# Forgetting attention of a decoder trunk: the queries' head norm moves from a multiply of the queries into the scale of the softmax exponential, and three query tiles move behind the first two heads' scores

## The chip, the cores and the metric

The kernel runs on one core of a Trainium2 chip. The metric is the device time of one execution in microseconds (us), lower is better. One core has a TensorE (PE, with its weight loads shown apart as PEld), a VectorE (DVE), a ScalarE (ACT), a GpSimd (POOL) and a SyncE (SP), which here issues nearly all DMAs in one queue. Each engine runs its own instructions strictly in the order in which they were written to it, and waits on semaphores for the others.

## The reference, cut to what matters

Two layers of a decoder trunk are computed for 512 prompt tokens and 8 x 4 sample tokens (T = 544 columns), width 1024, 8 heads of 128. The second layer mixes with forgetting attention:

```
q = rmsnorm((xn @ att_w_q).reshape(L, 8, 128), q_norm)      # per token and head
s = einsum('bqhd,bkhd->bhqk', q, k) * 128 ** -0.5
s = s + cq[..., :, None] - csum[..., None, :]               # running sums of log forget values
s = where(causal, s, -inf)
p = softmax(s, axis=-1)
o = einsum('bhqk,bkhd->bqhd', p, v);  mix = o @ att_w_o
```

The sample tokens do the same against 256 past keys per stream and their own 4 new ones, with the forget term as an additive bias.

## The kernel before

All activations lie transposed: 128 features on the partitions, 544 tokens along the free axis. A matrix product takes three passes (high part of the weights by high part of the input, high by low, low by high), so that products come out near fp32; `split_pair` and `prep` make the two parts of an activation (an ACT instruction for the high part, a DVE one for the low part). `ps` are PSUM tiles of two banks (three of them), `pb` tiles of one bank (two), `big` SBUF tiles of 128 x 2 x 544 (45 in a pool), `tmp` tiles of 128 x 544 (8).

The order of the work in the attention is a table, `ORDER`, of small steps; each letter is a function, each digit its head or group. A scheduler then places the instructions of each engine, using the table as priority. The steps that matter here:

- `qN` (`tile`): query tile of head N. Eight blocks of weights, 48 matmuls on 272 columns (L285, L289, L291) into a `ps`. `take` then multiplies by the token's norm on DVE (L1108) and squares on ACT (L786).
- `s0123`, `s4567` (`stat` before): the sums of squares of four heads by matmuls with a block of 32 ones (L794: 4 heads x 2 column halves per group, in fp32), an inverse square root on ACT (L385) with one correction on DVE (L388, L391, L392), four rows written to DRAM (L805) and read back spread over all partitions (L810, one DMA for each head).
- `nN` (`norm` before): DVE multiplies the head's query tile by the gain and that row (L1118).
- `pN` (`prep_q`): high and low part of the prompt columns of the query tile (L329, L330 on `big<-big`).
- `fN` (`fetch`): the head's keys and values from DRAM (L1153, L1154).
- `aN` (`qk`): scores in four blocks of 128 queries against 128 to 512 keys, in two `ps`: a matmul for the forget term (L1169, `L` times `R`), three for q times k (L1170, L1171, L1172) and one for the causal mask (L1174). Then for each block a maximum on DVE (L1184), exp with the maximum as bias and the row sum as second output on ACT (L1185), a reciprocal on DVE (L1186), and the normalisation on ACT for blocks 0 and 3 (L1190) and on POOL for blocks 1 and 2 (L1188).
- `tN` (`turn`): ten transposes of the probabilities (L1200) and their split. `vN` (`pv`): the product with the values (L1219 to L1221) and its split (L1224, L1225).
- `KN`, `VN`: two cache pages of a sample stream; `z` puts the sample queries into a zeroed tile (POOL, L1233), `S0`, `S1` the sample scores (L1246), `T`, `P`, `U`, `O` their softmax and values. `h..`, `o.` the output projection (L1330 to L1337).

The forget term is a matmul with 32 rows for each head: `terms`, made in the K/V stage by `forget`, go through DRAM and `fetch_terms` reads them back. Before, `L` (one tile for each of four heads, refilled for heads 4 to 7) holds the query side and `R` (one tile for all heads) the key side.

## Time and profile before

| what | value |
|---|---|
| median of 3 runs (lowest to highest) | 1928.19 us (1927.69 to 1928.4) |
| the profiled execution | 1928.06 us, of which the profile's span is 1926.3 us |
| busy: PE, DVE, ACT, POOL | 99%, 76%, 49%, 7% of the span |
| first query tile of the attention starts | about 1347.5 us into the span |
| first sample scores (L1246) | 1428.35 us |
| attention's last projections | about 1510 us |

A view named "windows" gives busy time in stretches of the span, "waits" who waited for whom, "timeline" merged instructions in order of time: start, duration, engine, line, operation, tiles, shapes, count, and in brackets the idle time of the engine just before and what ended it. [...] An fp32 matmul that isn't a transpose appears as two MATMUL records.

### The profile page before, as it was taken

The numbers are of one execution on the slowest core, as the hardware profiler recorded it, in microseconds if no ns is written. First come the engines' busy times: TensorE is split into PE (matmuls) and PEld (weight loads), VectorE is DVE, ScalarE is ACT, GpSimd is POOL, SyncE is SP. The second block draws the span as 40 slices with busy tenths as digits, with TensorE's granted clock in tenths as the row PEclk, the third lists the DMA queues.
The fourth block names the chain that finished last, engine by engine and source line by source line (L and its number), as shares of the span: only waits on it lengthen the run. The fifth ranks groups of instructions, "written<-read, shape, count | busy, mean of one in ns | idle before, by whom it ended". The sixth has DMA issues, their size and how long they took to land.

```text
span 1926.3 us, 39008 instructions
## 1 busy us (share of the span) xinstructions
PE 1904.8 (99%) x16508; PEld 1869.8 (97%) x16508; DVE 1457.4 (76%) x1799; ACT 949.2 (49%) x1396; POOL 143.4 (7%) x190
## 2 busy tenths in 40 slices
PE   9999999999999999999999999999999999999999
PEld 8999999999999999999999999999977899999999
DVE  7987877556788887767578887876476888878774
ACT  7544434424554544454466454444374754444461
POOL 0000000410100000023000000002131300000020
PEclk9999999999999999999999999999999999999999
DMA  5233234312223233431484232324769332332431
GB/s 196 90 102 121 89 118 156 99 48 88 89 88 116 91 115 120 132 112 46 149 305 150 98 129 71 128 95 128 226 214 332 99 110 84 109 113 86 140 108 47
DMA packets 98048, 237.62 MB, mean 123 GB/s; under 512 B 12130, under 2 KB 29826, under 8 KB 97874
## 3 DMA queue, kind: packets, MB, share of 16 engines
q1 hardware_dynamic: 97730, 235.09, 36.9%
q8 instruction: 130, 2.13, 0.5%
q14 instruction: 44, 0.36, 0.1%
q10 hardware_dynamic: 144, 0.04, 0.0%
HBM read 218.65 MB, written 16.44 MB: 122 GB/s over the span
## 4 chain that ended last, share of the span: by engine, by line
PE 89%; DVE 5%; ACT 2%; DMA 2%; issue 1%; SPq 0%; POOL 0%; ACTq 0%; DVEq 0%
PE ps L538 31%; PE ps L285 15%; PE ps L291 15%; PE ps L289 15%; PE pb L538 5%; DVE big L242 1%; DMA tmp<-rows 1%; ACT big L241 1%; PE ps L891 1%; PE ps L892 1%; PE ps L893 1%; DVE big L227 1%; DVE big L330 0%; PE ps L1285 0%; PE ps L676 0%
## 5 line engine op out<-in xcount | busy, mean ns | idle before, releaser
L538 PE MATMUL ps<-big,big 128*128 128x272 f32 x5616 | 668.5, 279 | 3.1 <-ACT tmp L546 1.7
L538 PEld LDWEIGHTS ps<-big,big 128*128 128x128 f32 x5616 | 658.4, 189 | 3.9 <-ACT tmp L546 2.1
L242 DVE TENSOR_TENSOR big<-big,big 128x1024 fp32r<-128x1024 f32 (+2 forms) x505 | 582.1, 1156 | 86.7 <-ACT big L241 85.9
L241 ACT CAST big<-big 128x1024 fp32r<-128x1024 f32 (+2 forms) x505 | 482.4, 975 | 325.1 <-DVE big L227 251.5
L285 PE MATMUL ps<-big,big 128*128 128x272 f32 x2668 | 530.1, 280 | 3.0 <-ACT big L241 1.4
L291 PE MATMUL ps<-big,big 128*128 128x272 f32 x2668 | 528.4, 279 | 2.9 <-DVE big L242 2.8
L289 PE MATMUL ps<-big,big 128*128 128x272 f32 x2668 | 527.5, 279 | 0.6 <-DVE big L342 0.6
L285 PEld LDWEIGHTS ps<-big,big 128*128 128x128 f32 x2668 | 407.2, 189 | 7.9 <-ACT big L241 4.5
L291 PEld LDWEIGHTS ps<-big,big 128*128 128x128 f32 x2668 | 406.9, 189 | 5.0 <-DVE big L242 4.5
L289 PEld LDWEIGHTS ps<-big,big 128*128 128x128 f32 x2668 | 406.9, 189 | 1.0 <-DVE big L342 1.0
L370 POOL TENSOR_TENSOR st<-st,tmp 128x544 f32<-128x544 f32 (+1 forms) x63 | 87.4, 1388 | 1472.4 <-ACT tmp L368 1472.1
L227 DVE TENSOR_TENSOR big<-big,big 128x1024 f32<-128x1024 f32 x156 | 190.1, 1219 | 0.0
L577 DVE SCALAR_TENSOR_TENSOR big<-ps,big 128x544 f32<-128x544 f32 x128 | 92.5, 722 | 104.1 <-PE ps L291 103.2
L546 ACT COPY tmp<-ps 128x544 f32<-128x544 f32 x117 | 71.5, 611 | 111.3 <-PE ps L538 111.3
L496 DVE TENSOR_TENSOR big<-big,st 128x1088 f32<-128x1088 f32 x88 | 113.5, 1291 | 3.3 <-ACT big L560 2.0
L538 PE MATMUL pb<-big,big 128*128 128x272 f32 x936 | 114.8, 279 | 0.0
L538 PEld LDWEIGHTS pb<-big,big 128*128 128x128 f32 x936 | 111.3, 189 | 0.0
L499 ACT ACTIVATE big<-big 128x544 f32<-128x544 f32 x88 | 57.8, 659 | 88.0 <-DVE big L496 87.9
L341 ACT ACTIVATE big<-big,gains 128x544 fp32r<-128x544 f32 (+1 forms) x80 | 55.4, 702 | 91.3 <-DVE big L577 55.2
L330 DVE TENSOR_TENSOR big<-big,big 128x544 fp32r<-128x544 f32 (+1 forms) x112 | 79.3, 714 | 22.7 <-ACT big L329 22.5
L342 DVE SCALAR_TENSOR_TENSOR big<-big,gains,big 128x544 fp32r<-128x544 f32 (+1 forms) x80 | 64.6, 817 | 24.3 <-ACT big L341 24.3
L329 ACT CAST big<-big 128x544 fp32r<-128x544 f32 (+1 forms) x112 | 71.2, 643 | 12.2 <-DVE big L502 7.4
(218 smaller groups left out, 1388.5 us busy)
## 6 DMA issues: line engine op xcount, KB each, us to landing
big<-in_w SPq DMA_DIRECT2D x156, 512.0 KB
big<-in_w2b SPq DMA_DIRECT2D x96, 384.0 KB
big<-in_w13p SPq DMA_DIRECT2D x16, 512.0 KB
big<-in_w2a SPq DMA_DIRECT2D x16, 512.0 KB
big<-in_win SPq DMA_DIRECT2D x16, 512.0 KB
big<-in_wg SPq DMA_DIRECT2D x16, 512.0 KB
big<-in_ck SPq DMA_DIRECT2D x16, 512.0 KB
big<-in_cv SPq DMA_DIRECT2D x16, 512.0 KB
```

Of the source, the lines that this page charges most:

```text
L227: self.nc.vector.tensor_tensor(t, a, b, ALU.add if op == "+" else ALU.subtract)
L241: self.nc.scalar.copy(hi, src)
L242: self.nc.vector.tensor_tensor(lo, src, hi.bitcast(F32), ALU.subtract)
L285: i = nc.tensor.matmul(o, wh, xh[:, b], start=s, stop=False)
L289: nc.tensor.matmul(o, wh, xl[:, b], start=False, stop=False)
L291: nc.tensor.matmul(o, wl, xh[:, b], start=False, stop=e)
L330: self.nc.vector.tensor_tensor(pair[:, 1, cols], src, pair[:, 0, cols].bitcast(F32), ALU.subtract)
L370: nc.gpsimd.tensor_tensor(acc[:, cols], acc[:, cols], sq, ALU.add)
L496: tt(g, g, rstd.unsqueeze(1).broadcast_to([P, 2, T]), ALU.mult)
L538: nc.tensor.matmul(turns(dst[w]), a[:, c], woven(b), start=k in "152" and kp == 0 and n == 0, stop=kp == NKP - 1 and n == 2, skip_group_ch ...
L546: nc.scalar.copy(t["r" + k], t["C" if k == "5" else "A"])
L577: nc.vector.scalar_tensor_tensor(halves(h[c]), whole(out), 0.5, halves(h[c]), ALU.mult, ALU.add)
```

## The change

The query tile is no longer normalised. `prep_q` now splits the raw query times the gain. The score matmuls then give q'k without the head norm y (y = 1 / sqrt(sum of squares + 128 eps), which holds the 128 ** -0.5 too), and the exponential multiplies by y, as a scale read per partition: in the scores, queries lie on the partitions. Since y multiplies the forget term as well, that term is divided by y beforehand: `L` holds 1/y of each token and head (high and low part), `R` the negative running sum, one tile for each of four heads.

To have y on the partitions, `stat(g)` takes the sums of squares as columns: for each of four heads and four blocks of 128 tokens one fp32 matmul with the squares as stationary operand and one column of ones as moving operand (L1122), and for group 1 two more for the sample tokens (L1125), whose squares POOL writes. One DVE chain of 15 dependent instructions on 128 x 16 (128 x 18) values follows (bit trick and three Newton steps, then 1/y and its high and low part), and two copies that spread these over a `tmp`. `rows(g)` (step `rN`) turns that by 16 fp32 matmuls with the identity (L1150) and copies it to `L` on ACT (L1152). The rows through DRAM and the eight multiplies of `norm` are gone. In the softmax, blocks go in pairs: two maxima, one multiply of both by the scale, two exps, one reciprocal for both. The gain of the sample queries is applied where they are put into the zeroed tile. Two cache pages (`K1`) are loaded later, and the query tiles 5, 6 and 7 stand after the rows of group 0 and between the first two heads' steps.

```
-q0 K3 K2 K0 q1 q2 q3 K1 s0123 n2 n3 n1 q4 f1 p1 q5 q6 f0 n0 q7 p2 p0 f3 f2 a0 s4567 p3 t0 a1 v0 a2
-t1 n4 n5 a3 n7 n6 t2 p4 z f4 K5 v1 v2 f5 p5 ...
+q0 K3 K2 K0 q1 q2 q3 s0 f0 q4 r0 p0 f1 q5 a0 p1 q6 t0 f2 a1 p2 q7 v0 s1 t1 p3 f3 a2 K1 r1 a3 t2
+p4 z f4 K5 v1 v2 f5 p5 ...
```

```
 forget:
-        act(t1[:, :SEQ], chf, AF.Identity, scale=role(4), bias=role(6))
-        act(t2[:, :SEQ], chf, AF.Identity, scale=role(2), bias=role(7))
-        dve.scalar_tensor_tensor(R[:, 0, :SEQ], clo[:, :SEQ], role(5), t1[:, :SEQ], ALU.mult, ALU.add)
-        dve.scalar_tensor_tensor(t2[:, :SEQ], clo[:, :SEQ], role(3), t2[:, :SEQ], ALU.mult, ALU.add)
+        act(t1[:, :SEQ], chf, AF.Copy, scale=role(4))
+        dve.scalar_tensor_tensor(t1[:, :SEQ], clo[:, :SEQ], role(5), t1[:, :SEQ], ALU.mult, ALU.add)
         for k in range(2):
-            act(L[:, k, :SEQ], t2[:, :SEQ], AF.Copy, scale=role(8 + k))
+            act(R[:, k, :SEQ], t1[:, :SEQ], AF.Copy, scale=role(8 + k))
 stat (new):
+            sq = sqs.pop(4 * g + j)
+            for i in range(4):
+                nc.tensor.matmul(t[:, 4 * j + i:4 * j + i + 1], sq[:, i * P:i * P + P], self.ones[:, 0:1], ...)
+        for k in range(2 * g):
+            nc.tensor.matmul(t[:, 16 + k:17 + k], ss[k], self.ones[:, 0:1], start=True, stop=True)
+        dve.tensor_scalar(x, t[:, :n], P * EPS, None, ALU.add)
+        dve.tensor_scalar(u.bitcast(I32), x.bitcast(I32), 1, None, ALU.logical_shift_right)
+        dve.tensor_scalar(y.bitcast(I32), u.bitcast(I32), -1, 0x5f3759df, ALU.mult, ALU.add)
+        for _ in range(3):
+            dve.tensor_tensor(u, y, y, ALU.mult)
+            dve.scalar_tensor_tensor(u, u, -0.5, x, ALU.mult, ALU.mult)
+            dve.scalar_tensor_tensor(y, u, 1.5, y, ALU.add, ALU.mult)
...
 rows (new):
+        for i in range(4):
+            for j in range(4):
+                nc.tensor.matmul(t[32 * j:32 * j + 32, i * P:i * P + P], w[:, 128 * j + 32 * i:128 * j + 32 * i + 32],
+                                 self.ident, start=True, stop=True, skip_group_check=True)
+        nc.scalar.copy(self.L[:, g, :SEQ], t)
 softmax, block i of head h:
+                if i % 2 == 0:
+                    m2, l2, r2 = self.sm(2), self.sm(2), scale[:, 4 * h + i:4 * h + i + 2]
+                    for k in range(2):
+                        nc.vector.tensor_reduce(m2[:, k:k + 1], S[i // 2][:, k, :w + P * k], AX.X, ALU.max, negate=True)
+                    nc.vector.tensor_tensor(m2, m2, r2, ALU.mult)
-                nc.scalar.activation(blocks_halves(p[:, :w]), blocks_unwoven(sc), AF.Exp, bias=m, accum_out=l)
+                nc.scalar.activation(blocks_halves(p[:, :w]), blocks_unwoven(sc), AF.Exp, bias=m2[:, k], scale=r2[:, k],
+                                     accum_out=l2[:, k])
```

How the instructions move. Rows give line, operation, written tile, read tiles, shape and count; lines of the changed kernel are higher by some 35. On PE, where the fourth query tile ends (its tile is `ps_16502` in both), before:

```order
L291 MATMUL ps_16502<-big_16218,big_16377 128x272 x2
L794 MATMUL pb_16577<-tmp_16385,ones 32x272
L794 MATMUL pb_16577<-tmp_16437,ones 32x272
L794 MATMUL pb_16577<-tmp_16494,ones 32x272
L794 MATMUL pb_16578<-tmp_16385,ones 32x272
L285 MATMUL ps_16615<-big_15943,big_16439 128x272 x2
```

and now, with the fifth query tile in `ps_16601`, its last passes, and the sixth tile in `ps_16687`:

```order
L1122 MATMUL pb_16556<-ones,tmp_16379 128x1 x4
L1122 MATMUL pb_16556<-ones,tmp_16433 128x1 x4
L1122 MATMUL pb_16556<-ones,tmp_16492 128x1 x4
L285 MATMUL ps_16601<-big_15937,big_16437 128x272 x2
...
L1122 MATMUL pb_16556<-ones,tmp_16552 128x1 x4
...
L291 MATMUL ps_16601<-big_16212,big_16438 128x272 x2
L1150 MATMUL pb_16656<-consts,tmp_16588 32x128 x16
L285 MATMUL ps_16687<-big_15937,big_16496 128x272 x2
```

The fourth head's columns stand ten passes into the fifth query tile, and the turn of group 0 (L1150) stands between the fifth and the sixth.

On PE at the second group, before: the last group of ones (L794) stands around the first scores (`ps_16871`, `ps_16872`), ahead of them all:

```order
L1169 MATMUL ps_16872<-big_16225,big_16228 128x384
L794 MATMUL pb_16922<-tmp_16790,ones 32x272
L794 MATMUL pb_16923<-tmp_16790,ones 32x272
L794 MATMUL pb_16922<-tmp_16855,ones 32x272
L794 MATMUL pb_16923<-tmp_16855,ones 32x272
L1170 MATMUL ps_16871<-big_16792,big_16860 128x256
```

and now: the columns of group 1, head 1's transposes (L1241), the scores of heads 2 and 3 (`ps_17074`, `ps_17075` and `ps_17162`, `ps_17163`), the turn of group 1, and head 2's transposes:

```order
L1122 MATMUL pb_17006<-ones,tmp_16986 128x1 x4
L1125 MATMUL pb_17006<-ones,big_16220 128x1 x2
L1241 MATMUL ps_17043<-consts,tmp_16908 128x128
...
L1202 MATMUL ps_17074<-big_16222,big_16219 128x256
...
L1207 MATMUL ps_17163<-neg,identr 128x256
L1150 MATMUL pb_17144<-consts,tmp_17040 32x128 x16
L1241 MATMUL ps_17209<-consts,tmp_17102 128x128
```

The turn of group 1 now stands on PE between the scores of head 3 and the transposes of head 2; no query tile is left behind it.

On DVE in the same stretch, before, maxima, reciprocals and splits follow each other, with one head norm (L1118) among them:

```order
L1225 TENSOR_TENSOR big_17036<-pb_17023,big_17036 128x512
L330 TENSOR_TENSOR big_17102<-ps_17090,big_17102 128x512
L330 TENSOR_TENSOR big_17104<-pb_17091,big_17104 128x256
L1184 TENSOR_REDUCE sm_17143<-ps_17120 128x1
L1186 RECIPROCAL sm_17084<-sm_17084 128x1
L1118 SCALAR_TENSOR_TENSOR big_16664<-big_16664,gains,tmp_17114 128x544
L330 TENSOR_TENSOR big_17103<-ps_17090,big_17103 128x384
```

and now (`cols` is the tile of the chain; nine of its 15 steps stand ahead of these rows):

```order
L330 TENSOR_TENSOR big_17056<-ps_17043,big_17056 128x384
L1219 TENSOR_TENSOR sm_17097<-sm_17097,cols 128x2
L1132 TENSOR_TENSOR cols<-cols 128x18
L342 SCALAR_TENSOR_TENSOR big_17067<-big_16490,gains,big_17067 128x512
L330 TENSOR_TENSOR big_17057<-pb_17044,big_17057 128x128
L1133 SCALAR_TENSOR_TENSOR cols<-cols 128x18
L1134 SCALAR_TENSOR_TENSOR cols<-cols 128x18
L1138 TENSOR_TENSOR cols<-cols 128x16
L1139 CAST cols<-cols 128x16
L1140 TENSOR_TENSOR cols<-cols 128x16
L1144 COPY tmp_17040<-cols 128x128x2
L1218 TENSOR_REDUCE sm_17109<-ps_17075 128x1 x2
```

The chain of group 1 is mixed with the splits of head 1 and the maxima of head 2, and the maxima of head 2's second half (`ps_17075`) stand behind its last step and the first of its two copies.

## The prediction

> **What bounds the kernel now.** I read the page first, then busy time by stretches, then who waits for whom, then PE's instructions in order of time in the attention.

> ```profile
> span 1926.3 us, 39008 instructions
> PE 1904.8 (99%) x16508; PEld 1869.8 (97%) x16508; DVE 1457.4 (76%) x1799; ACT 949.2 (49%) x1396; POOL 143.4 (7%) x190
> PE 89%; DVE 5%; ACT 2%; DMA 2%; issue 1%; SPq 0%; POOL 0%; ACTq 0%; DVEq 0%
> ```

> TensorE is the bound: it is busy 99% of the span and carries 89% of the chain that ended last. A change can win only what PE does, or the little time in which PE waits. The stretches (duration; busy time and count of PE, PEld, DVE, ACT, POOL; granted clock; DMA share; GB/s) show where that is:

> ```profile
> 1347.50:1369.74 22.24, 22.24 (x193) 22.11 (x192) 10.91 (x14) 9.79 (x13) 4.78 (x10) 1.00 0.99 271
> 1369.74:1428.35 58.61, 54.59 (x402) 47.72 (x401) 35.41 (x77) 32.25 (x77) 12.47 (x26) 1.00 0.49 161
> 1428.35:1510.00 81.65, 78.94 (x818) 66.38 (x818) 58.95 (x121) 48.43 (x123) 27.00 (x55) 1.00 0.85 286
> ```

> The first row is the first four query tiles: no wait at all, 22.24 us / 193 passes = 0.115 us a pass, so 5.55 us for a tile of 48. The second goes from there to the first sample scores and holds all that the change moves: four query tiles, the scores of heads 0 to 4, transposes of heads 0 to 3, values of heads 0 to 2. Both orders have exactly this work ahead of the sample scores, so I make the sum at that point. PE idles 4.0 us there. The third stretch keeps its work and order and idles 2.7 us.

> The waits in the second stretch, and the longest wait of the DMA queue there:

> ```profile
> DVE big L1118 <- DMA tmp<-rows: 2.7, 4, 1.1
> PE ps L1169 <- ACT tmp L1185: 2.1, 3, 1.3
> SPq L805 <- DVE st L392: 12.5, 2, 12.2
> ```

> PE does not wait for the head-norm rows through DRAM as such; it waits for exponentials to free PSUM (L1169 waiting for L1185). And the queue's 12 us stand, where the row writes block it, makes no row in which PE waits for a DMA. In order of time on PE:

> ```profile
> 1369.74 1.12 PE L794 MATMUL pb<-tmp,ones 128*32 128x272 f32 x12
> 1370.79 0.50 PE L285 MATMUL ps<-big,big 128*128 128x272 f32 x2
> 1373.65 1.10 PE L794 MATMUL pb<-tmp,ones 128*32 128x272 f32 x4
> 1388.90 1.11 PE L794 MATMUL pb<-tmp,ones 128*32 128x272 f32 x8
> 1390.00 0.50 PE L285 MATMUL ps<-big,big 128*128 128x272 f32 x2
> 1396.72 1.10 PE L794 MATMUL pb<-tmp,ones 128*32 128x272 f32 x4
> 1398.13 1.10 PE L794 MATMUL pb<-tmp,ones 128*32 128x272 f32 x4 [0.31 <-ACT tmp L786]
> 1402.72 0.33 PE L1200 MATMUL ps<-consts,tmp 128*128 128x128 f32 x1 [0.71 <-ACT tmp L1190]
> 1406.16 0.43 PE L1169 MATMUL ps<-big,big 128*128 128x384 f32 x1 [1.29 <-ACT tmp L1185]
> 1411.58 0.43 PE L1169 MATMUL ps<-big,big 128*128 128x384 f32 x1 [0.53 <-ACT tmp L1185]
> 1417.24 0.43 PE L1169 MATMUL ps<-big,big 128*128 128x384 f32 x1 [0.32 <-ACT tmp L1185]
> ...
> 1419.29 0.93 PE L1200 MATMUL ps<-consts,tmp 128*128 128x128 f32 x7
> 1419.98 0.46 PE L1219 MATMUL pb<-big,big 128*128 128x512 f32 x1
> ...
> 1428.35 1.52 PE L1246 MATMUL pb<-big,big 128*32 128x128 f32 x48
> ```

> Five blocks of ones cost about 1.05 us each to the next start (1369.74 to 1370.79, 1388.90 to 1390.00). Then, with the query tiles used up, the first heads' softmax is exposed: the waits in brackets.

> **The change part by part.**

> *Removed on PE:* the ones, 5 x 1.05 = 5.2 us, all on the path.

> *Added on PE:* 34 column matmuls (16 + 18) with 128 x 128 stationary squares and one moving column, and 32 matmuls of 32 output rows by 128. Both forms stand in the trace, the first in the K/V stage (four matmuls, eight records), the second in the sample scores:

> ```profile
> 915.40 1.02 PE L864 MATMUL pb<-consts,st 128*128 128x1 f32 x8 [0.57 <-DVE st L392]
> 916.36 0.24 PE L866 MATMUL pb<-consts,st 128*32 128x1 f32 x8
> 916.53 0.50 PE L285 MATMUL ps<-big,big 128*128 128x272 f32 x2
> 1456.80 3.75 PE L1246 MATMUL pb<-big,big 128*32 128x128 f32 x128
> 1460.49 0.55 PE L1200 MATMUL ps<-consts,tmp 128*128 128x128 f32 x3
> ```

> Eight records of the first form take 916.36 - 915.40 = 0.96 us, 0.12 each; 34 matmuls are 68 records: 8.2 us. The second: (1460.49 - 1456.80) / 128 = 0.029 each; 64 records: 1.9 us. They stand in PE's order between other work, so all of it is on the path. With one moving column it is the loading of 128 stationary columns that costs: with 32 stationary columns (L866) eight take 0.17 us. [...]

> PE work so: -5.2 + 8.2 + 1.9 = +4.9 us.

> *Waits that go.* Sixth and seventh tile now stand behind head 0's scores and the eighth behind head 1's. What head 0's transposes wait for:

> ```profile
> 1407.89 0.27 PE L1174 MATMUL ps<-neg,identr 128*128 128x256 f32 x1
> 1409.23 0.59 ACT L1185 ACTIVATE tmp<-ps,sm 128x384 f32<-128x384 f32 x1
> 1410.32 1.24 POOL L1188 TENSOR_SCALAR tmp<-tmp,sm 128x384 f32<-128x384 f32 x1 [0.47 <-DVE sm L1186]
> ```

> From a head's last score (1408.0) to its slowest normalised block (1411.56) is 3.6 us, less than a tile's 5.55, even with the pairing (one more maximum and a multiply, some 0.6 us) and the table load for exp. So heads 0 and 1 wait for nothing. What that returns lies between 4.0 us (PE's idle time) and 7.6 us (58.6 us less the work at its pace: 4 tiles x 5.55, 5 heads' scores of 6656 columns x 2.8, 4 x 10 transposes x 0.1 to 0.11, 3 values of 4224 columns x 1.8, and 5.2 of ones make 51.0; columns at 0.115 us for 272, transposes by 0.69 us for the seven at 1419.29), since the start-to-start gaps around a wait are longer than its idle time. I take 5.5, a little under the middle, since part of the difference (the 0.50 instead of 0.40 us of the first pass behind an fp32 matmul, above) stays.

> *The chain on DVE, group 0.* The nearest rows are the log-sigmoid's, on 128 x 40:

> ```profile
> 933.84 1.37 DVE L988 SCALAR_TENSOR_TENSOR tmp<-tmp 128x40 f32<-128x40 f32 x6
> 935.71 0.24 DVE L993 COPY tmp<-tmp 128x160 f32<-128x160 f32 x1
> 947.38 0.75 DVE L1032 SCALAR_TENSOR_TENSOR sm<-sm,consts,sm 128x8 f32<-128x8 f32 x3
> ```

> 0.23 to 0.25 us a dependent step; 15 steps 3.5 us, two copies 0.6: 4.1. On PE, 24 column records (2.9), ten passes (1.15) and 8 records (0.96) put the sums at 1374.8 on the old clock; the chain ends at 1379.0. The fifth tile's other 38 passes end at 1379.1. So the turn of group 0 waits 0 to 0.4 us; its cover is these 4.4 us, and it has no slack.

> *The chain of group 1* has no query tile behind it. I put PE's and DVE's orders side by side, from the end of the 18 columns (0), with these rows:

> ```profile
> 1404.62 0.67 DVE L1184 TENSOR_REDUCE sm<-ps 128x1 f32<-128x512 f32 x1
> 1409.36 0.69 DVE L330 TENSOR_TENSOR big<-ps,big 128x512 fp32r<-128x512 f32 x1 [0.54 <-ACT big L329]
> 1410.63 0.41 DVE L330 TENSOR_TENSOR big<-pb,big 128x256 fp32r<-128x256 f32 x1
> 1410.75 0.69 ACT L1185 ACTIVATE tmp<-ps,sm 128x512 f32<-128x512 f32 x1 [0.18 <-DVE sm L1184]
> ```

> PE: head 1's transposes to 1.1, head 2's scores to 3.95. DVE: seven steps to 1.6, then splits of head 1 mixed with steps and maxima of head 2; the split that frees a PSUM tile for head 3 ends at 4.1 to 4.4 (PE waits 0.2 to 0.7), the exps that free the next let PE wait 0.25 to 0.35. Last steps, first copy, second maxima of head 2, second copy: 8.0 to 8.4. PE is at the turn at 7.2 to 7.6 and waits 0.8 to 0.9. Head 2's second exps begin only then; its third block leaves POOL at 11.4 to 12.1, PE is there at 9.5: 2.1 to 2.3 us. Head 3's follow in the same queues: 0.85 to 1.4. Together 4.2 us with the starts from row to row, 5.7 with full durations. On DVE an instruction here starts some 0.08 us before the one ahead of it ends (1404.62 + 0.67 against the next at 1405.21), so I take 4.2; the bounds are 0 (all hidden) and 6.1 (with the first chain's 0.4).

> *At nothing:* DVE loses eight multiplies (L1118, 0.78 each), two corrections and 16 reciprocals and gets the chains and 16 small multiplies; all beside PE, except as counted above. ACT swaps four root instructions for two copies of 128 x 512. POOL gets 32 small squares and a multiply for each copy; it is busy 12.5 of 58.6 us. SP loses 16 DMAs and its 12 us stand, and gets `K1`'s two pages behind head 3's keys; DMA is at 0.49 there and the pages have a head's scores and more before their use. Should that cover fail, a wait for a page at the sample scores would follow; it is in the range's upper end. The forget term's edit saves an ACT and a DVE instruction beside the K/V stage's matmuls.

> Sum: +4.9 - 5.5 + 4.2 = +3.6 us on the profiled execution's 1928.06 (1926.3 of span): 1931.66, say **1931.6 us**. The median, 1928.19, is 0.13 above that execution, which changes nothing.

> **The rivals.**
> 1. *The second chain hides.* If ACT's and POOL's queues let head 2's early blocks through, PE waits 1 us or less instead of 4.2: 1928.4, range 1926 to 1929.6. For it: ACT is busy only 32 of 58.6 us. Against it: the maxima stand behind the chain on DVE, whatever ACT does.
> 2. *Both chains are late.* The upper ends, 6.1 us, and head 2's lateness passes to heads 4 and 5, where PE has idled 0.49 us before: 1934 to 1938. It decides once a step takes over 0.25 us.
> 3. *The columns are cheap* (ends on the other side). If a stationary load hides behind the matmul ahead of it, a record costs what L866 shows, 0.021 us: 1.4 us instead of 8.2, and the second chain begins earlier: 1923 to 1924.5, faster from a record price of about 0.01 to 0.02 us on. Against it: L864's 0.12, in the very form. [...]

> **How the numbers follow.** What a measurement here tells from no change is about 0.2%, 3.9 us: below 1924.3 is faster, above 1932.05 slower. The forecast's case (1929.6 to 1934) has 0.44, of which 0.24 ends within 0.2% and 0.20 above; rival 1 has 0.24, all within; rival 2 has 0.24, all slower; rival 3 has 0.08, faster. So faster 0.08, same 0.48, slower 0.44. The range 1926 to 1936 leaves out rival 3 and the upper half of rival 2.

> **What would show it.** L1122 with L1125 at about 8.2 us and L1150 at about 1.9 us of PE's time; no PE wait before the transposes of heads 0 and 1; the turn of group 0 waiting under 0.5 us, that of group 1 near 0.8, both for DVE's copies; then head 2's third block on POOL as PE's longest wait of the stretch; the sample scores at about 1432 us; the stretch from there to the last projection 81 to 82 us as before. I am wrong if a column record takes well under 0.12 us, if PE waits for a page or for keys, or if the stretch behind the sample scores changes by over 1.5 us.

## The result and the profile after

| kernel | median (runs, lowest to highest), us | against the kernel before in the same set |
|---|---|---|
| before | 1927.68 (8, 1926.9 to 1928.4) | |
| changed | 1935.18 (8, 1930.46 to 1936.34) | 1.0034 [1.0025, 1.0043] |
| changed, a second set of runs | 1931.9 (8, 1930.96 to 1935.2) | 1.0025 [1.0015, 1.0036] |

The change makes the kernel slower by 0.25 to 0.34%. The forecast was 1931.6 us, the range 1926 to 1936. In the first set the kernel before keeps within 1.5 us (over all sets 103 of its 104 runs lie between 1926.5 and 1929.0 us, one at 1930.29); the changed one spreads over 6 us, and that spread is the larger part of the story.

The changed kernel's profiled execution took 1935.55 us, with a span of 1933.8. The head of its page, the busy times and the chain that ended last:

```profile
span 1933.8 us, 39207 instructions
PE 1913.1 (99%) x16608; PEld 1884.2 (97%) x16608; DVE 1453.6 (75%) x1816; ACT 949.4 (49%) x1393; POOL 149.7 (8%) x206
PE 90%; DVE 5%; ACT 2%; issue 1%; DMA 1%; SPq 0%; POOL 0%; ACTq 0%; DVEq 0%; POOLq 0%
```

PE is busy 8.3 us longer, though the change added only some 4 us of PE work. The stretches that answer to the first two of before (duration; busy time and count of PE, PEld, DVE, ACT, POOL; granted clock; DMA share; GB/s):

```profile
1347.04:1369.28 22.24, 22.24 (x194) 22.24 (x193) 11.11 (x14) 9.80 (x13) 9.49 (x21) 1.00 0.97 286
1369.28:1436.51 67.23, 64.13 (x502) 61.32 (x500) 33.69 (x99) 32.68 (x75) 15.09 (x35) 0.90 0.44 136
```

The four query tiles take 22.24 us as before. The stretch from there to the first sample scores grew from 58.61 to 67.23 us while PE's idle time in it fell from 4.02 to 3.10 us. The new thing stands in the clock's column: 0.90 in the place of 1.00. PE's timeline at group 0's sums (start, duration, engine, line, operation, count):

```profile
1369.28 2.73 PE L1122 MATMUL pb<-ones,tmp 128*128 128x1 f32 x24
1371.88 0.48 PE L285 MATMUL ps<-big,big 128*128 128x272 f32 x2
...
1373.20 1.70 PE L1122 MATMUL pb<-ones,tmp 128*128 128x1 f32 x8
1374.76 0.80 PE L291 MATMUL ps<-big,big 128*128 128x272 f32 x2
1375.35 0.66 PE L285 MATMUL ps<-big,big 128*128 128x272 f32 x2
1375.81 0.66 PE L289 MATMUL ps<-big,big 128*128 128x272 f32 x2
...
1381.83 1.08 PE L1150 MATMUL pb<-consts,tmp 128*32 128x128 f32 x32
1382.84 0.50 PE L285 MATMUL ps<-big,big 128*128 128x272 f32 x2
```

The first 24 column records take 2.60 us to the next start, 0.108 each. The next eight take 1.56 us, 0.195 each, and the ordinary passes behind them start every 0.23 us (1375.35 to 1375.81 for two), twice the 0.115 of before: TensorE runs at half clock. The same trace cut where the clock steps:

```profile
1369.66:1373.07 3.41, 3.41 (x32) 3.41 (x32) 0.55 (x1) 0.66 (x1) 0.99 (x4) 0.99 0.46 180
1373.07:1379.85 6.78, 6.78 (x32) 6.78 (x32) 3.04 (x17) 0.00 (x0) 0.00 (x0) 0.50 0.00 0
1407.18:1410.59 3.41, 3.41 (x32) 3.41 (x31) 1.42 (x2) 1.13 (x2) 1.64 (x7) 1.00 0.78 289
1410.59:1417.41 6.82, 6.82 (x34) 6.82 (x34) 2.35 (x10) 1.33 (x4) 0.00 (x0) 0.50 0.01 2
```

Twice the clock is halved for 6.8 us, each time behind 3.41 us that are mostly one-column matmuls. In all these rows PE counts as busy without a gap. PE does in such a stretch what takes half of it at full clock, so the loss is 3.4 us each time, 6.8 us together. Group 1 and the waits behind it:

```profile
1408.22 4.68 PE L1122 MATMUL pb<-ones,tmp 128*128 128x1 f32 x32
1412.76 0.99 PE L1125 MATMUL pb<-ones,big 128*128 128x1 f32 x4
...
1422.63 1.08 PE L1150 MATMUL pb<-consts,tmp 128*32 128x128 f32 x32
1424.45 0.55 PE L1241 MATMUL ps<-consts,tmp 128*128 128x128 f32 x3 [0.73 <-ACT tmp L1222]
1426.05 0.44 PE L1241 MATMUL ps<-consts,tmp 128*128 128x128 f32 x2 [1.06 <-POOL tmp L1230]
...
1429.84 0.66 PE L1241 MATMUL ps<-consts,tmp 128*128 128x128 f32 x4 [0.56 <-POOL tmp L1230]
...
1436.51 3.75 PE L1288 MATMUL pb<-big,big 128*32 128x128 f32 x128
...
1527.34 0.28 PE L1378 MATMUL ps<-big,big 128*128 128x272 f32 x1
```

No wait of 0.2 us or more stands ahead of the transposes of heads 0 and 1; those that are left stand at the transposes of heads 2 and 3 and the values behind them. The turn of group 1 (1422.63) waits for nothing, because PE came to it late. The sample scores begin at 1436.51, 8.2 us later than before. From there to the last projection pass it is 1527.34 - 1436.51 = 90.83 us; before:

```profile
1520.03 0.28 PE L1335 MATMUL ps<-big,big 128*128 128x272 f32 x1
```

1520.03 - 1428.35 = 91.68 us. The rest of the program is the same in both.

### The profile page after: what moved, and what is told of

Its sections match the earlier page's. It is cut to its first block, busy times and chain, and to the rows that moved or that the text cites. A ratio compares the mean times of both kernels' runs of the same rounds, so it can differ in the third digit from the quotient of the medians.

```text
span 1933.8 us, 39207 instructions
## 1 busy us (share of the span) xinstructions
PE 1913.1 (99%) x16608; PEld 1884.2 (97%) x16608; DVE 1453.6 (75%) x1816; ACT 949.4 (49%) x1393; POOL 149.7 (8%) x206
## 4 chain that ended last, share of the span: by engine, by line
PE 90%; DVE 5%; ACT 2%; issue 1%; DMA 1%; SPq 0%; POOL 0%; ACTq 0%; DVEq 0%; POOLq 0%
PE ps L538 31%; PE ps L285 15%; PE ps L291 15%; PE ps L289 15%; PE pb L538 5%; DVE big L242 1%; PE ps L891 1%; ACT big L241 1%; PE ps L892 1%; PE ps L893 1%; DVE big L227 1%; DVE big L330 0%; PE pb L1122 0%; PE ps L1328 0%; ACT tmp L1222 0%
## 5 line engine op out<-in xcount | busy, mean ns | idle before, releaser
L285 PE MATMUL ps<-big,big 128*128 128x272 f32 x2668 | 531.5, 280 | 3.9 <-ACT big L241 2.7
L285 PEld LDWEIGHTS ps<-big,big 128*128 128x128 f32 x2668 | 408.7, 190 | 7.7 <-ACT big L241 5.1
L341 ACT ACTIVATE big<-big,gains 128x544 fp32r<-128x544 f32 (+2 forms) x88 | 61.1, 704 | 90.4 <-DVE big L577 55.1
L342 DVE SCALAR_TENSOR_TENSOR big<-big,gains,big 128x544 fp32r<-128x544 f32 (+2 forms) x88 | 70.5, 809 | 25.4 <-ACT big L341 25.3
L330 DVE TENSOR_TENSOR big<-big,big 128x544 fp32r<-128x544 f32 (+1 forms) x104 | 73.8, 716 | 20.4 <-ACT big L329 20.3
L329 ACT CAST big<-big 128x544 fp32r<-128x544 f32 (+1 forms) x104 | 66.3, 645 | 8.6 <-DVE big L502 7.4
```

Source lines behind the costliest of these rows:

```text
L285: i = nc.tensor.matmul(o, wh, xh[:, b], start=s, stop=False)
L330: self.nc.vector.tensor_tensor(pair[:, 1, cols], src, pair[:, 0, cols].bitcast(F32), ALU.subtract)
```

## The experiments

The half clock could be the cause or a bystander. In the rows above it comes for 6.78 and 6.82 us, twice 3.41, each time behind 3.41 us that are mostly one-column matmuls. Theory 1, a guess from those rows: the blocks bring it. Their records load weights all the time (PEld 3.41 of 3.41 us), but move one column each, and whatever sets the granted clock, called the gate here, might not count that as work. A window below is such a stretch of 3.41 us ahead of or behind a step of the clock. Theory 2: PE's added work and the waits behind the second chain make the time. Each kernel was timed beside the kernel before on the same chip, but not all on one chip, so small differences between them are read from the ratios. The medians:

| kernel | us (runs, lowest to highest) | ratio to before |
|---|---|---|
| spread | 1929.62 (11, 1929.38 to 1930.82) | 1.0013 [1.0004, 1.0022] |
| wide | 1929.55 (11, 1929.18 to 1930.51) | 1.0011 [1.0002, 1.002] |
| narrow | 1932.77 (8, 1931.0 to 1933.99) | 1.0027 [1.0017, 1.0038] |
| block | 1930.76 (11, 1929.64 to 1931.83) | 1.0019 [1.001, 1.0028] |
| order | 1936.82 (5, 1936.55 to 1938.06) | 1.0051 [1.0037, 1.0065] |
| old_order | 1928.95 (11, 1928.52 to 1930.94) | 1.001 [1.0001, 1.0019] |
| later | 1929.9 (11, 1929.43 to 1930.85) | 1.0012 [1.0003, 1.0021] |
| single | 1926.79 (11, 1926.23 to 1927.42) | 0.9998 [0.9989, 1.0007] |
| both | 1926.62 (11, 1925.46 to 1927.01) | 0.9993 [0.9984, 1.0002] |
| single_old | 1927.31 (11, 1926.24 to 1928.9) | 1.0 [0.9991, 1.0009] |
| full | 1926.4 (11, 1925.74 to 1927.83) | 0.9995 [0.9986, 1.0004] |

### Columns taken apart

```
-q0 K3 K2 K0 q1 q2 q3 s0 f0 q4 r0 p0 f1 q5 a0 p1 q6 t0 f2 a1 p2 q7 v0 s1 t1 ...
+q0 K3 K2 K0 q1 c0 q2 c1 q3 c2 c3 s0 f0 q4 r0 p0 f1 q5 a0 c4 p1 q6 t0 c5 f2 a1 c6 p2 q7 v0 c7 s1 t1 ...
```

(`cN` issues the four column matmuls of head N, `sN` keeps the rest; lines are higher by four.)

> The changed kernel with the columns of sums taken apart: each head's four one-column matmuls (eight records, 0.87 us) stand behind a query tile, the scores or the transposes, where the changed kernel has them in blocks of 24, 8 and 36 records. Same number of instructions. [...] Theory 2 (work and waits): the time comes from PE's added records and the waits behind the second chain, and the clock is by the way: 1934 to 1936 us.

1929.62 us, well below theory 2's 1934 to 1936, so theory 1. The same instructions take 5.6 us less than in the first set of the changed kernel, and 2.3 us less than in the second. Its runs spread over 1.4 us, those of the changed kernel over 5.9 in the first set. The stretch, on its clock:

```profile
1369.28:1430.76 61.48, 58.02 (x503) 54.86 (x501) 33.28 (x99) 32.80 (x75) 16.63 (x35) 1.00 0.51 155
```

PE's timeline now shows the second chain's waits as they are at full clock:

```profile
1416.88 1.08 PE L1154 MATMUL pb<-consts,tmp 128*32 128x128 f32 x32 [0.66 <-DVE sm L1223]
1418.71 0.55 PE L1245 MATMUL ps<-consts,tmp 128*128 128x128 f32 x3 [0.74 <-ACT tmp L1226]
1420.31 0.44 PE L1245 MATMUL ps<-consts,tmp 128*128 128x128 f32 x2 [1.06 <-POOL tmp L1234]
...
1424.91 0.40 PE L1206 MATMUL ps<-big,big 128*128 128x384 f32 x1 [0.23 <-DVE big L330]
1425.88 0.45 PE L1264 MATMUL pb<-big,big 128*128 128x512 f32 x1 [0.57 <-DVE big L330]
```

and DVE's, what the turn waits for:

```profile
1415.18 0.33 DVE L1148 COPY tmp<-cols 128x256 f32<-128x256 f32 x1
1415.39 1.15 DVE L1222 TENSOR_REDUCE sm<-ps 128x1 f32<-128x384 f32 x2
1416.45 0.28 DVE L1148 COPY tmp<-cols 128x256 f32<-128x256 f32 x1
```

The second copy stands behind head 2's maxima; the profile puts the wait down to a small multiply behind it (L1223). 0.66 us stands where the prediction had 0.8 to 0.9.

### More columns through the array, same blocks

```
-nc.tensor.matmul(t[:, 4 * j + i:4 * j + i + 1], sq[:, i * P:i * P + P], self.ones[:, 0:1],
+nc.tensor.matmul(t[:, 4 * j + i:4 * j + i + P], sq[:, i * P:i * P + P], self.onesr[:].bitcast(F32),
...
```

> The changed kernel with 128 moving columns of ones in the place of one (the results of neighbours overwrite all but the first column), in the same blocks. Theory 1 (the gate goes by what moves through the array): clock 1.00, a record still 0.11 us since its weight load takes that long anyway, 1929.5 to 1932 us. Theory 1b (the gate drops for something else in these blocks, the weight loads or the idle DMA): half clock as in the changed kernel, 1934 to 1937 us. If moving columns and loads add up, a record takes about 0.16 to 0.21 us, and the time is 1933 to 1937 us with the clock at 1.00.

1929.55 us, theory 1 again, and this is the cleanest test: the blocks and their weight loads stay, only what moves is changed (and with it what is written to PSUM; the two are not told apart). PE's timeline:

```profile
1369.40 2.84 PE L1122 MATMUL pb<-onesr,tmp 128*128 128x128 f32 x24
1371.99 0.48 PE L285 MATMUL ps<-big,big 128*128 128x272 f32 x2
```

24 records take 2.59 us: 128 columns cost what one does, 0.108 us a record. That the price is the weight load's is an inference from the kernel before, where one-column records cost 0.12 us with 128 stationary columns (L864) and 0.021 us with 32 (L866). In the stretches there is a third effect:

```profile
1373.00:1376.00 3.00, 3.00 (x29) 3.00 (x28) 1.41 (x8) 0.00 (x0) 0.00 (x0) 1.00 0.00 0
1416.43:1419.84 3.41, 1.71 (x37) 1.12 (x35) 2.14 (x9) 3.39 (x11) 2.14 (x2) 1.00 1.13 312
1419.84:1423.25 3.41, 3.33 (x12) 3.06 (x13) 0.86 (x3) 3.41 (x10) 1.76 (x3) 0.50 1.13 338
```

Behind the blocks the clock stays at 1.00 with the DMA as idle (0.00) as in the changed kernel, so idle DMA isn't the cause. But the waits at head 2's transposes leave PE busy for 1.71 of 3.41 us, and the next 3.41 us run at half clock: here it follows waits. So 'wide' is not at full clock throughout. That it takes as long as 'spread' is in part chance: this half clock costs it 1.7 us, but PE idles 2.08 us ahead of its sample scores and 3.46 us in 'spread'.

> The changed kernel with 16 moving columns of ones in the place of one, in the same blocks. [...] If the gate only looks for instructions that move next to nothing: full clock, 1929.5 us as 'wide'.

(The edit is that of 'wide', with 16 columns.) 1932.77 us, not the 1929.5 of full clock; the runs beside it of the changed kernel itself lie at 1931.9. Group 1's block was followed by 6.8 us at half clock, group 0's was not, though other passes had only 1.24 of the 3.42 us ahead (1372.03 to 1373.27). The windows behind the two, group 0's first:

```profile
1373.42:1376.83 3.41, 3.41 (x33) 3.41 (x32) 2.15 (x13) 0.00 (x0) 0.00 (x0) 1.00 0.00 0
1407.55:1410.96 3.41, 3.41 (x18) 3.41 (x18) 0.38 (x3) 0.00 (x0) 0.00 (x0) 0.50 0.02 5
```

In the changed kernel 1.19 us of other passes ahead (1371.88 to 1373.07), beside one-column records, were followed by half clock. Whether the 16 columns or the 0.05 us make the difference isn't shown.

### The same kernel again

> The changed kernel once more, unchanged, with its own five rounds beside 'narrow'. [...] If the extra time is fixed work and waits: all runs at 1935 whatever the clock.

The time follows the clock. All 16 runs of the changed kernel, by the mean granted clock that stands with each:

| clock | us |
|---|---|
| 0.999 | 1930.46, 1930.52, 1930.96 |
| 0.998 | 1932.18 |
| 0.997 | 1931.37, 1931.58, 1931.67, 1932.13, 1932.42, 1933.3 |
| 0.996 | 1934.86, 1935.2, 1935.52 |
| 0.995 | 1935.51, 1935.55, 1936.34 |

The profile of this second set, a run of 1932.42 us, shows one way in which they differ:

```profile
1371.79:1375.21 3.42, 3.42 (x31) 3.42 (x31) 0.14 (x1) 0.14 (x1) 0.46 (x2) 1.00 0.15 56
1405.93:1409.34 3.41, 3.41 (x33) 3.41 (x33) 0.69 (x1) 0.88 (x2) 1.44 (x7) 1.00 0.48 169
1409.34:1416.17 6.83, 6.83 (x32) 6.83 (x32) 3.72 (x17) 2.12 (x6) 0.00 (x0) 0.50 0.00 0
```

What stood in the 3.41 us ahead, by the profiles. Beside one-column records, other passes had 1.19 us (1371.88 to 1373.07) and 1.04 us (1407.18 to 1408.22) in the changed kernel, 1.06 us in 'block' (1382.24 to 1383.30, below) and none in the second set's group 1; each time half clock followed. In the second set's group 0 they had 1.55 us (1372.85 to 1374.09 and 1374.90 to 1375.21), and full clock stayed. Where PE waited in the attention, half clock followed 0.36 us of busy PE ('order'), 1.51 ('single'), 1.62 ('old_order'), 1.63 ('single_old') and 1.71 ('wide'), and did not follow 1.81 and 1.84 ('order'). Elsewhere the same figures don't part the cases: at the program's start half clock followed 1.57 us (first profile) and 2.24 (second set), but not 2.11 ('single'), and near the end of the kernel before 1.62 us (1920.77 to 1924.18) kept full clock. So these are the rows of this case, and what is counted isn't shown; PE's busy time as the profile gives it is not all of it, since it is 3.41 of 3.41 us ahead of both steps of the changed kernel. The half clock lasted two windows where the first of them still held one-column or 16-column records (both groups of the first profile, group 1 of the second and of 'narrow'), and one in 'block', where it held none.

### The price of a block by itself

```
 stat, before:
+            if hs[0] == 0:
+                t = self.pb()
+                for j, sq in enumerate(sq4):
+                    for i in range(4):
+                        nc.tensor.matmul(t[:, 4 * j + i:4 * j + i + 1], sq[:, i * P:i * P + P], self.ones[:, 0:1], ...)
+                nc.vector.tensor_copy(self.sm(8), t[:, 8:16])
```

> The kernel before with 16 one-column matmuls (32 records) added in one block inside the sixth query tile, their result not used, and one copy of 8 columns on DVE. Their price alone: 32 x 0.108 = 3.5 us, 1931.2 us (theory 2, and theory 1 where a window's border falls in the middle of the block). Theory 1 where a window holds most of the block: half clock for 6.8 us behind it, 3.4 us more, 1934.6 us; most runs near that, some lower, and the mean clock at 0.998.

1930.76 us: 3.4 us more than before, which by the numbers I had written is the price without the gate. The profile, of a run of 1929.73 us, near the fastest, says otherwise:

```profile
1378.75 3.63 PE L1119 MATMUL pb<-ones,tmp 128*128 128x1 f32 x32
```

```profile
1379.89:1383.30 3.41, 3.41 (x32) 3.41 (x32) 0.17 (x1) 0.00 (x0) 0.00 (x0) 1.00 0.96 225
1383.30:1386.71 3.41, 3.41 (x17) 3.41 (x17) 1.60 (x3) 0.00 (x0) 0.75 (x2) 0.50 0.85 320
```

The clock does drop, to 0.50 for one window, 3.41 us, and not two: the block ends at 1382.24 us, ahead of the step at 1383.30, the half-clock window holds query tile passes alone, and at 1386.71 the clock is back. The loss is 1.7 us and not 3.4. And PE's idle time ahead of the sample scores fell from 4.02 to 2.56 us, so the later waits took part of the block's price. The blocks of ones (L794) also moved: they stand in four groups here and in five before, of some 1.05 us each, be they of 4, 8 or 12 records, so this run has one such price less. The expectation was wrong in both sizes; the time alone could not have told the theories apart, the clock behind the block does.

### The order

```
-q0 K3 K2 K0 q1 q2 q3 K1 s0123 n2 n3 n1 q4 f1 p1 q5 q6 f0 n0 q7 p2 p0 f3 f2 a0 s4567 p3 t0 a1 v0 a2
-t1 n4 n5 a3 n7 n6 t2 p4 ...
+q0 K3 K2 K0 q1 q2 q3 s0123 f0 q4 n0 p0 f1 q5 a0 n1 p1 q6 t0 f2 a1 n2 p2 q7 v0 s4567 t1 n3 p3 f3 a2 K1 a3 t2
+n4 n5 n6 n7 p4 ...
```

> The kernel before, with its head norm through DRAM rows, in the changed kernel's order: query tiles 5, 6 and 7 behind the rows of group 0 and the first two heads' scores, the second page load late. By the prediction's term for the waits that go (5.5 us, bounds 4.0 to 7.6): 1920 to 1924 us, 1922.2 at the middle. Rival: the head norm's rows now come too late for the scores of head 0, whose norm no longer has three tiles behind it, and PE waits for the exponentials later instead: 1926 to 1929 us. The clock is 1.00 in both.

1936.82 us, far outside both numbers. Who waits between the fourth query tile and the sample scores:

```profile
DVE big L1118 <- DMA tmp<-rows: 6.5, 3, 5.2
PE pb L1200 <- DVE tmp L391: 3.1, 1, 3.1
PE ps L1200 <- ACT tmp L1185: 2.8, 1, 2.8
```

With rows through DRAM this order puts a 5.2 us wait for a row into DVE's queue, and transposes behind the root's correction of group 1 (L391); PE idles 11.6 us ahead of the sample scores, and behind them 10.2 us run at half clock, which the expectation had excluded. So with rows through DRAM the order loses, and this run says nothing on what it is worth with the new head norm. That is the next one, on top of 'wide':

> The kernel 'wide' (new head norm, columns with 128 moving ones, so at full clock) in the order of the kernel before: sixth to eighth query tile ahead of the first scores, the second page load early. By the prediction's terms (5.5 us of waits that the new order takes away, 4.2 us that it brings): 1.3 us more than 'wide', 1930.8 us; by PE's idle time ahead of the sample scores (4.02 us before, 2.08 us in 'wide'): 1931.5 us, with PE waiting for head 0's exponentials again near 1404 us. Rival: the order is worth nothing, 1929.5 us.

1928.95 us: with the new norm the old order is no worse; by the ratios (1.0010 and 1.0011) the two are the same. Six of its runs lie at 1928.5 to 1929.0 us with a clock of 1.000, five at 1930.0 to 1930.9 with 0.998 or 0.999. The profiled one, 1930.31 us, is of the second kind. PE's waits ahead of the sample scores in it:

```profile
PE ps L1202 <- ACT tmp L1222: 1.8, 1, 1.8
PE ps L1241 <- ACT tmp L1222: 1.1, 1, 1.1
PE pb L1260 <- DVE big L330: 0.6, 1, 0.6
```

3.5 us: 1.8 at head 2's scores, for the exponentials of a head ahead of it, 1.1 at head 2's transposes and 0.6 at values. The first is followed by one window of half clock (1409.59 to 1413.00 us). 'spread' has 3.46 us, at the turn of group 1 and behind it. With the new norm both orders wait about as long, in different places.

```
 later (on top of wide):
-... q7 v0 s1 t1 p3 f3 a2 K1 r1 a3 t2 p4 z f4 K5 v1 v2 ...
+... q7 s1 v0 t1 p3 f3 a2 K1 a3 v1 r1 t2 p4 z f4 K5 v2 ...
```

> The kernel 'wide' with head 0's values behind group 1's columns and head 1's values ahead of group 1's turn, so that two value products (some 1.15 us each) stand beside group 1's chain and ahead of head 2's transposes. If the waits there (2.1 us of PE's idle time in 'wide', more by start-to-start gaps) come from that chain, as the prediction says: 1.5 to 2.5 us less, 1927 to 1928 us. Rival: the same time is waited later, for head 3's softmax: 1929 to 1930 us.

1929.9 us, no gain: the rival held in its time. The transposes of head 2 waited less (0.30 us), and the scores of the next heads for exponentials instead (2.4 us in two waits).

### Looking for a version that beats both

```
 single (on top of wide; results on even columns):
-                q[h], sqs[h] = qc, self.square(qc)
+                q[h], sqs[h] = qc, self.tmp(F32R)
+                nc.scalar.activation(sqs[h], qc, AF.Square)
...
```

> The kernel 'wide' with the squares written as fp32r, so that a column matmul is one record and not two (32 + 4 records in the place of 68; the sums are less exact). At 0.108 us a record, 32 fewer: 3.5 us less, 1926.0 us, if a record's price is its weight load. If the price goes by the matmul, not by the record (0.216 us in both formats), no change: 1929.5 us. If the half of it in group 1 turns into waits for the chain there: 1927.7 us.

1926.79 us, 2.8 of the 3.5 us; between the full price and the case in which group 1's half turns into waits, and nearer to the first. PE's timeline:

```profile
1369.36 1.45 PE L1123 MATMUL pb<-onesr,tmp 128*128 128x128 f32 x12
1370.65 0.45 PE L285 MATMUL ps<-big,big 128*128 128x272 f32 x2
```

12 records in 1.29 us, 0.107 each, where the fp32 records of 'wide' take 0.108: the price goes by the record, and an fp32 column matmul, with two of them, pays it twice.

> 'later' and 'single' together. If both hold and add up: 1923.5 to 1925 us, below both kernels by 0.1 to 0.2%. If the second chain's waits take what the columns give: 1926 to 1927.5 us.

1926.62 us: the two don't add up, as 'later' alone brought nothing.

> 'single' (one record per column matmul) in the order of the kernel before. If the new order is worth nothing, as 'old_order' says (1928.95 against 1929.55 us), and the 3.5 us of column records come off in full: 1925.5 to 1926.2 us, below the kernel before by 0.1%. If the new order helps where the columns are short: 1927 to 1928 us.

1927.31 us, no better than 'single'. Its runs lie between 1926.24 us at a clock of 1.000 and 1928.9 at 0.998, and its profile has a window in which PE truly waits (1.63 of 3.41 us busy), with half clock behind it:

```profile
1403.92:1407.33 3.41, 1.63 (x15) 1.24 (x18) 3.26 (x13) 2.31 (x8) 0.00 (x0) 1.00 0.10 22
1407.33:1410.74 3.41, 3.41 (x40) 3.02 (x38) 0.76 (x2) 2.39 (x8) 0.92 (x1) 0.50 0.03 7
```

> 'both' with 256 moving columns of ones in the place of 128 in its one-record column matmuls, so that columns move all through a record's 0.107 us. 'both' lies in two groups of runs, 1925.5 to 1925.8 and 1926.6 to 1927.0 us; if the upper group is still the gate (128 fp32r columns move for half of a record), all runs come to 1925.5 to 1925.8 us, 0.1% below the kernel before. If the upper group comes from elsewhere: 1926.6 us as 'both'. If 256 columns no longer hide behind the weight load: some 0.02 to 0.1 us a record more, 1927 to 1930 us.

1926.4 us, with runs from 1925.74 to 1927.83 and no gap between two groups, so this does not settle what the upper group of 'both' was. Its clocks fit windows at half clock (1.000 in all four lower runs, 0.998 or 0.999 in six of the seven upper ones); the profiled run, 1927.01 us, is the seventh and has no half clock. 256 columns no longer hide: 12 records take 1.41 us, 0.118 each.

The intervals of 'single', 'both' and 'full' all hold 1: with columns of half the price the new head norm comes level with the old one, and no version here is shown to beat the kernel before.

## Why the prediction was right or wrong

The range held, the sum behind it did not, and that the range held is luck. Without the half clock behind the columns ('spread', 'wide') the kernel takes 1929.6 us, 2.2 to 2.3 us above the kernel before in the same set, where the prediction had 3.6. The half clock adds another 5.6 us (first set) or 2.3 us (second). The two errors point in opposite directions, and in the second set they nearly cancel: 1931.9 us beside a forecast of 1931.6. The upper end of the range, in which the first set's 1935.18 us lies, was there for chains later than forecast or a late page, and neither came.

- **The step that failed:** "They stand in PE's order between other work, so all of it is on the path." The records' own time was on the path, as said; what they do to the work behind them was not in the sum: twice 6.8 us at half clock, a loss of up to 6.8 us. All rows quoted had a granted clock of 1.00, and the sum took it as given. The row that gave the price, L864, is a block of eight records, 0.96 us, under a third of 3.41 us, and it shows no drop.
- **The columns** were priced at 0.12 us a record, 8.2 us. At full clock they take 0.108, 7.4 us. Rival 3 (0.021 us a record) is out.
- **The turns**: 1.01 us each (1381.83 to 1382.84), 2.0 us against 1.9. PE work at full clock so +4.2 us, not +4.9.
- **Group 0's chain**: no wait at the turn, as said, in 'wide' and 'spread' too, where PE is at full clock there. Its steps start 0.21 us apart, not 0.23 to 0.25, and rival 2, which begins at 0.25, falls with its mechanism, although its range of 1934 to 1938 holds the first set's median.
- **Group 1's chain**: at full clock the order of waits is the predicted one: 0.66 us at the turn (0.8 to 0.9), 0.74 + 1.06 at head 2's transposes with POOL's block the longest (2.1 to 2.3), 0.23 + 0.57 in the work behind (0.85 to 1.4 at head 3): 3.3 against 4.2 us. The 0.45 to 1.05 us that the prediction had ahead of head 3's scores did not come. Rival 1's time, up to 1929.6, is what the kernel does at full clock, but not for its reason: the chain doesn't hide.
- **The waits that go**: heads 0 and 1 wait for nothing, as said. What that returned can be estimated from the stretch's sum: in 'spread' it is 2.9 us longer than before, with 4.2 of PE work and 3.5 of waits added, which leaves 4.8 us; in 'wide' (60.99 us to the sample scores, 2.1 of waits, 1.7 of half clock) 5.6 us. So 5.5 fits. But it isn't the order's gain, as the prediction had it: by 5.5 and 4.2 the new order should win 1.3 us, and 'old_order' against 'wide' shows none.
- **Behind the sample scores** nothing was to change; it takes 0.85 us less there (90.83 against 91.68), in 'spread' and 'wide' as well, and in 'old_order' (90.80), so neither the order nor the late pages make it. Why isn't settled. The 81 to 82 us of the prediction end at 1510 us; the last projection pass of before starts at 1520.03.
- **The late pages** cost nothing: no wait for a DMA of 0.2 us or more stands in PE's rows of that stretch.

## What to carry to other kernels

Read the granted clock's column in every stretch that a change touches, and when an edit adds a block of matmuls with few moving columns, look for a step of the clock behind it: here three of the four blocks in the changed kernel's two profiles, and the one in 'block', were followed by 3.4 or 6.8 us at half clock, and such a block's price was its records plus half of that. Here such a block could be taken apart ('spread', 1929.62 us), or given more moving columns: 128 cost 0.108 us a record like one ('wide'), while 256 in one-record matmuls cost 0.118 where 128 cost 0.107 ('full', 'single'). And where a kernel's runs spread more than its predecessor's, look at the clock that stands with each run before looking for work in the median.

## What the runs showed of the hardware that was not expected

- TensorE at half clock, 0.50, for 6.8 us twice in the changed kernel's first profile, behind windows in which PE was busy for 3.41 of 3.41 us, mostly with one-column matmul records of 0.108 us.
- Half clock behind waits as well: in the attention it followed 0.36 to 1.71 us of busy PE in 3.41 us in five runs' profiles, and not 1.81 or 1.84 in one; at the program's start it followed 2.24 us once.
- The same program took 1930.5 to 1936.3 us, with the clock that stands with each run (0.999 to 0.995); its two profiles have the steps of the clock at different places in the blocks.
- A record with 128 fp32 moving columns costs as much as with one: 0.108 us ('wide').
